# A small matrix product without a reader moves from the edge of a tile to its middle

## The chip, the cores and the metric

The kernel runs on one core of a Trainium2 chip. The metric is device time in microseconds (us) of one execution; the median of the runs before is 1422.33 us (three runs, 1422.17 to 1423.14).

## The reference

Two transformer blocks on 256 tokens of width 1024, in fp32. The parts that matter here:

```python
def first_block(...):            # attention, RG-LRU, merge, feed-forward
    xn = rmsnorm(h, norm_mix_g[l])
    u = jnp.einsum('bsd,de->bse', xn, w_in[l])
    ...
    r = jax.nn.sigmoid(jnp.einsum('bsnd,nde->bsne', xb, w_r).reshape(B, S, D) + b_r)
    i = jax.nn.sigmoid(jnp.einsum('bsnd,nde->bsne', xb, w_i).reshape(B, S, D) + b_i)
    ...
    g, up = jnp.split(hn @ w_ffn_in[l], 2, axis=-1)
    h = h + (jax.nn.silu(g) * up) @ w_ffn_out[l]
...
def swiglu(h, w_in, w_out):      # four more feed-forward layers in the second block
    gate, up = jnp.split(h @ w_in, 2, axis=-1)
    return (jax.nn.silu(gate) * up) @ w_out
```

In the second block stand, in this order, a feed-forward layer, a spatial gating unit (its `u` and `v` come out of one product, `v` is normalised and mixed over 128 tokens), two feed-forward layers, an attention with stick-breaking weights, and a last feed-forward layer.

## The kernel before

Every large product is made of three products on TensorE: weights and activations are each split into a high and a low part of type fp32r (`h`, `l` and `xh`, `xl`), and `mm3` (lines 213 to 216) adds high by high, high by low and low by high into one bank of the accumulation memory. In the trace these three are named by what they read: `xh,h`, `xl,h` and `xh,l` in the tiles that run over the input width, and `rr,h`, `rr,h`, `rr,l` where the activations lie in the tiles `rr`. Each of them is a weight load of 128x128 (engine PEld in the profile) and a matmul that streams 256 columns (engine PE). A weight tile of 128 by 1024 thus gives 24 products; a group is two tiles (`group`, line 200), 48 products.

There are five feed-forward layers, called f0 to f4 (`ffn`, line 738). Each begins with four chunks in K order (96 products) for the first two pairs of gate and up columns, then goes through the list of `ffn_order`: G2, G3, G4, R0, G5, G6, R1 and so on. G is a group of a gate tile and an up tile (`pe_a`, line 229); R is a group of two row tiles of the output product (`pe_r`, line 238). f4 makes its output in token order, with 512 columns a product (`pe_rn`). The bank of each G is read by `mulR` (line 314), which scales it on VectorE, then by silu, product and split.

The normalisation's factor comes in beside the running products: `stats_a` (line 296) sums squares with fp32 products of one column (`ones` by the tile `sb`), `stats_b` (line 305) broadcasts the factor with two fp32 products (`bcast_mm`). In f0, f2, f3 and f4 `stats_a` stands after the first tile of G2 and `stats_b` after the first tile of G3. f1 has two factors: sums after the first tile (`early`) and after the second tile (`sa`, in the trace `ones,sd`) of G2, and two broadcasts one behind the other in `sbb`.

`nudge` (line 292) is a bf16 product of 64 rows and 32 columns, of a part of an identity matrix with itself. Its result has no reader. One stands at the end of every `stats_b` (and of the second broadcast in f1), one behind the last `mix` of the spatial gating, and one wherever `due` is set when `pe_a` begins a first tile (lines 231 to 233): at G5 of every feed-forward layer (line 772), and after the last of the gate products of `lru` (line 659), which are fp32. That last one stands ahead of a tile of the first block's input product; 288 products of that kind follow it, and then a stage of 512-column products. The columns that it writes are those where the tile's own first product then starts anew.

The order on each engine is the order in which the code calls it; nothing reorders it. Banks come from two pools of four, `wk` and `acc`, in rotation: a call of `wk()` hands out the bank used four calls before, and its first writer waits for that bank's last reader. Weights come with DMAs of 1 MB on SP's queue, three ahead, and are split on ScalarE (line 163) and VectorE (line 164) up to seven tiles ahead.

Of the kernel before, what the change touches and what calls it, by code (L numbers as in the profile page):

```python
# [39 lines left out]
def ffn_order():  # L40
    seq, j, r = [("G", 2), ("G", 3), ("G", 4), ("R", 0)], 5, 1
    while j < NJ:
        for _ in range(2):
            if j < NJ:
                seq.append(("G", j))
                j += 1
        seq.append(("R", r))
        r += 1
    return seq + [("R", i) for i in range(r, NJ // 2)]
# [57 lines left out]
class Builder:  # L107
    def __init__(self, tc, dram, pools):
        self.tc, self.nc, self.dram = tc, tc.nc, dram
        self.cp, self.rawp, self.hlp, self.accp, self.wkp = pools  # L110
        self.ci = 0
        self.preps = 0
        self.loads = 0
        self.raw = {}
        self.hl = {}
        self.gens = []
        self.R = None
        self.rcol = None
        self.due = False

    @property
    def gi(self):
# [87 lines left out]
    def mm(self, out, lhsT, rhs, start, stop):  # L210
        self.nc.tensor.matmul(out, lhsT, rhs, start=start, stop=stop, skip_group_check=True)  # L211

    def mm3(self, out, wh, wl, xh, xl, start, stop):
        self.mm(out, wh, xh, start, False)
        self.mm(out, wh, xl, False, False)
        self.mm(out, wl, xh, False, stop)

    def pe_k(self, h, l, kp, xs, outs):
        XH, XL = xs
# [8 lines left out]

    def pe_a(self, h, l, xs, out, first):
        XH, XL = xs  # L230
        if first and self.due:
            self.nudge(out[:, 0:32], True)
            self.due = False
        for k in range(8):
            s = slice(k * 128, k * 128 + 128)
            self.mm3(out, h[:, s], l[:, s], XH[:, k, :], XL[:, k, :], start=(first and k == 0), stop=(k == 7))

    def pe_r(self, h, l, zh, zl, accs, first, last):
# [50 lines left out]
            self.mm(bank[:, half, t * 128:(t + 1) * 128], col[:, t:t + 1].to_broadcast([128, 128]), self.ident,  # L289
                    start and t == 0, True)  # L290

    def nudge(self, out, start=False):

        self.mm(out, self.identb[0:64, :], self.identb[0:64, 0:32], start, True)

    def stats_a(self, pool=None, kv=False):

# [316 lines left out]
    def lru(self, xr, xc, rt, it, gr, gb, ga, gw):  # L614
# [4 lines left out]
        def conv(k):  # L619
            nc.scalar.activation(xc[:, k, :], xr[:, k, 0:256], AF.Identity, bias=P("conv_b", k), scale=P("conv_w", k))  # L620
            for j in range(1, 4):
                nc.vector.scalar_tensor_tensor(xc[:, k, :], xr[:, k, j:j + 256], P("conv_w", 8 * j + k), xc[:, k, :],
                                               op0=ALU.mult, op1=ALU.add)
# [30 lines left out]
        for p in range(4):  # L654
            banks = [self.acc(), self.acc()]
            for wi in range(2):
                for f in range(2):
                    self.mm(banks[wi][:, f, :], gw[:, wi * 8 + 2 * p + f, :], xc[:, 2 * p + f, :], f == 0, True)
            self.due = p == 3
            if p < 2:  # L660
                conv(2 * p + 4)
            yield
            for f in range(2):
                k = 2 * p + f
                nc.scalar.activation(rt[:, k, :], banks[0][:, f, :], AF.Sigmoid, bias=P("b_r", k))
            yield
            if p < 2:
                conv(2 * p + 5)
            yield
            for f in range(2):  # L670
                k = 2 * p + f
                nc.scalar.activation(it[:, k, :], banks[1][:, f, :], AF.Tanh, bias=self.half[:, k:k + 1], scale=0.5)
            yield
            sl = slice(2 * p, 2 * p + 2)
            nc.vector.scalar_tensor_tensor(it[:, sl, :], it[:, sl, :], 1.0, xc[:, sl, :], op0=ALU.add, op1=ALU.mult)
# [10 lines left out]
        for i in range(2):  # L686
            s = slice(i * 1024, (i + 1) * 1024)
# [4 lines left out]
        for i in range(2):  # L692
            s = slice(i * 1024, (i + 1) * 1024)
# [44 lines left out]
    def ffn(self, n, fin, fin_l, stats=None, nat=False, more=None):  # L738
        nc = self.nc
        a, r = ("A", f"{n}_in"), ("R", f"{n}_out")  # L740
        HH, HL = self.RR[0], self.RR[1]
        tmp = [self.SA[:, i * 512:(i + 1) * 512].rearrange("p (a b) -> p a b", b=256) for i in range(4)]

        def ev(j, bank):
            t = tmp[j % 4]
            self.mulR(t, bank)
            yield
            nc.scalar.activation(t[:, 0, :], t[:, 0, :], AF.Silu)  # L748
            yield
            if nat:  # L750
                nc.vector.scalar_tensor_tensor(t[:, 1, :], t[:, 0, :], 0.5, t[:, 1, :], op0=ALU.mult, op1=ALU.mult)
            else:
                nc.vector.tensor_tensor(t[:, 1, :], t[:, 0, :], t[:, 1, :], op=ALU.mult)  # L753
            yield
            self.hl_split(t[:, 1, :], HH[:, j % 8, :], HL[:, j % 8, :])
            yield

        b = [self.wk(), self.wk()]
        self.start_k((("K", f"{n}_in"),) * 2, [b[0][:, 0, :], b[0][:, 1, :], b[1][:, 0, :], b[1][:, 1, :]],
                     ((2, 2), (0, 0)) if more else ((2, 2), (2, 2)))  # L760
        sa, sbb = stats or (self.stats_a, self.stats_b)

        def first():
            sbb()
            for j in range(3):
                self.spawn(ev(j, b[j]))

        accs = None
        for kind, i in ffn_order():
            if kind == "G":  # L770
                bank = self.wk()
                self.due = i == 5
                if i == 2:
                    b.append(bank)
                self.group((a, a), lambda c, h, l, s: self.pe_a(h, l, self.XS, bank[:, c, :], c == 0),
                           mid={2: sa, 3: first}.get(i), fills=(0, 1) if more and i < 4 else (2, 2),
                           end=more if i == 2 else lambda: self.spawn(ev(i, bank)))
            elif i < NJ // 2 - 1:
                if accs is None:
                    accs = self.ffn_accs(nat)  # L780
                self.group((r, r), lambda c, h, l, s: (self.pe_rn if nat else self.pe_r)(
                    h, l, HH[:, s[2] % 8, :], HL[:, s[2] % 8, :], accs, not nat and s[2] == 0, False))
        zf = lambda k: (HH[:, k % 8, :], HL[:, k % 8, :])
        if nat:
            self.tail_nat(f"{n}_out", (NJ - 2, NJ - 1), zf, accs, fin)
        else:
            self.tail_group(f"{n}_out", (NJ - 2, NJ - 1), zf, accs, lambda p: fin(p, accs[p]), fin_l)
# [571 lines left out]
```

## Time and profile before

| | |
|---|---|
| median of three runs | 1422.33 us |
| the profiled execution | 1422.0 us |
| its span, first to last instruction | 1420.3 us |
| mean granted TensorE clock | 0.999 |
| TensorE matmuls, busy | 1410.6 us (99%), 11564 records |
| TensorE weight loads, busy | 1368.7 us (96%), 11564 records |
| VectorE, busy | 949.8 us (67%) |
| ScalarE, busy | 735.0 us (52%) |
| DMA | 260.31 MB, 183 GB/s |

Busy time of a matmul overlaps that of the next (a record of a 256-column product lasts some 0.28 us, while the next begins much earlier), so 99% says that TensorE nearly always has work, not how fast it goes through it. How fast is read from starts: from the count of records in a stretch, or from the timeline.

### The profile page before, as it was taken

To read this page: it belongs to the slowest core of one execution; us is meant where nothing else is said; L and a number is where in the kernel's file an instruction comes from. 1 tells how busy PE (TensorE), PEld (TensorE's weight loads), DVE (VectorE), ACT (ScalarE), POOL (GpSimd) and SP (SyncE) were. 2 spreads that over 40 slices of the span, in tenths; PEclk is the share of its full clock that TensorE was granted. 3 is DMA by queue.
4 is the path that set the end of the run, shared out by engine and by line. 5 is a ranking of instruction groups with operands and counts; after the bars stand their busy time and mean duration, and the time that the engine had idled before them with its cause. 6 is when DMAs were issued, how large, how long until landed. Compare 5 with 4: busy or idle time off the path is not lost.

```text
span 1420.3 us, 26991 instructions
## 1 busy us (share of the span) xinstructions
PE 1410.6 (99%) x11564; PEld 1368.7 (96%) x11564; DVE 949.8 (67%) x1316; ACT 735.0 (52%) x1094; POOL 24.7 (2%) x57
## 2 busy tenths in 40 slices
PE   9999999999999999999999999999999999999998
PEld 9998999999999999998999999999999998999997
DVE  6976687665567666677785665667665677656663
ACT  5686465544445445455445444446544477544442
POOL 0000000000000000000000000000000000000000
PEclk9999999999999999999999999999999999999999
DMA  8555554555544555556445554454555552445551
GB/s 299 192 198 197 176 189 154 203 195 191 179 178 149 206 182 206 203 198 223 160 156 183 186 206 179 178 188 169 208 184 211 199 179 90 161 152 197 190 187 51
DMA packets 37624, 260.31 MB, mean 183 GB/s; under 512 B 4224, under 2 KB 4608, under 8 KB 7040
## 3 DMA queue, kind: packets, MB, share of 16 engines
q1 hardware_dynamic: 36288, 253.77, 50.1%
q0 software_dynamic: 1072, 4.72, 1.0%
q8 instruction: 90, 1.47, 0.4%
q14 instruction: 30, 0.25, 0.1%
q10 hardware_dynamic: 144, 0.10, 0.0%
HBM read 257.53 MB, written 1.05 MB: 182 GB/s over the span
## 4 chain that ended last, share of the span: by engine, by line
PE 98%; DMA 0%; ACT 0%; DVE 0%; SPq 0%; issue 0%; POOLq 0%; POOL 0%
PE wk L211 62%; PE acc L211 36%; DMA raw<-w 0%; PE acc L530 0%; PE wk L530 0%; ACT sf L971 0%; ACT sd L961 0%; DVE l L164 0%; ACT h L163 0%; SPq L361 0%; SPq L352 0%; DVE sf L962 0%; POOLq L1355 0%; POOL rc L284 0%; ACT sh L1148 0%
## 5 line engine op out<-in xcount | busy, mean ns | idle before, releaser
L164 DVE TENSOR_TENSOR l<-raw,h 128x1024 fp32r<-128x1024 f32 (+1 forms) x479 | 571.3, 1220 | 241.3 <-ACT h L163 240.9
L211 PE MATMUL wk<-xh,h 128*128 128x256 f32 x2272 | 637.5, 281 | 1.4 <-ACT h L163 1.4
L211 PE MATMUL wk<-xh,l 128*128 128x256 f32 x2272 | 633.5, 279 | 0.1
L211 PE MATMUL wk<-xl,h 128*128 128x256 f32 x2272 | 633.2, 279 | 0.0
L163 ACT ACTIVATE h<-raw 128x1024 fp32r<-128x1024 f32 (+1 forms) x479 | 486.3, 1046 | 61.3 <-PE acc L211 28.0
L211 PEld LDWEIGHTS wk<-xh,h 128*128 128x128 f32 x2272 | 430.8, 190 | 4.5 <-issue 2.0
L211 PEld LDWEIGHTS wk<-xh,l 128*128 128x128 f32 x2272 | 427.7, 188 | 0.5 <-DVE l L164 0.5
L211 PEld LDWEIGHTS wk<-xl,h 128*128 128x128 f32 x2272 | 427.6, 188 | 0.5
L211 PE MATMUL acc<-rr,h 128*128 128x256 f32 x2016 | 353.5, 279 | 0.0
L211 PEld LDWEIGHTS acc<-rr,h 128*128 128x128 f32 x2016 | 306.1, 189 | 2.1 <-issue 1.9
L211 PE MATMUL acc<-rr,l 128*128 128x256 f32 x1008 | 280.4, 278 | 0.0
L211 PEld LDWEIGHTS acc<-rr,l 128*128 128x128 f32 x1008 | 189.3, 188 | 0.0
L748 ACT ACTIVATE sa<-sa 128x256 f32<-128x256 f32 x110 | 45.4, 417 | 258.5 <-DVE sa L315 258.3
L318 ACT ACTIVATE rr<-sa 128x256 fp32r<-128x256 f32 (+1 forms) x122 | 52.7, 439 | 185.3 <-DVE sa L753 128.9
L315 DVE TENSOR_TENSOR sa<-wk,rt 128x512 f32<-128x512 f32 x92 | 62.4, 687 | 72.5 <-PE wk L211 54.8
L319 DVE TENSOR_TENSOR rr<-sa,rr 128x256 fp32r<-128x256 f32 (+1 forms) x122 | 54.1, 451 | 53.4 <-ACT rr L318 53.4
L211 PE MATMUL acc<-h,rr 128*128 128x512 f32 (+1 forms) x208 | 63.1, 374 | 0.0
L211 PEld LDWEIGHTS acc<-h,rr 128*128 128x128 f32 x208 | 38.5, 188 | 6.6
L262 ACT ACTIVATE xh<-x,par 128x256 fp32r<-128x256 f32 x56 | 25.0, 501 | 29.4 <-DVE x L325 16.2
L211 PE MATMUL acc<-l,rr 128*128 128x512 f32 (+1 forms) x104 | 39.0, 375 | 0.0
L753 DVE TENSOR_TENSOR sa<-sa 128x256 f32<-128x256 f32 x88 | 37.1, 429 | 0.0
L211 PE MATMUL wk<-rr,h 128*128 128x256 f32 x192 | 33.0, 277 | 0.0
(255 smaller groups left out, 972.8 us busy)
## 6 DMA issues: line engine op xcount, KB each, us to landing
raw<-w SPq DMA_DIRECT2D x237, 1024.0 KB, 5.0
sd<-bias POOLq DMA_DIRECT2D x8, 384.0 KB, 3.4
raw<-w SPq DMA_DIRECT2D x3, 512.0 KB, 7.6
sh<-gates SPq DMA_DIRECT2D x1, 1024.0 KB, 9.1
out<-sf SPq DMA_DIRECT2D x4, 256.0 KB, 2.2
x<-x SPq DMA_DIRECT2D x3, 256.0 KB, 6.6
raw<-w SPq DMA_DIRECT2D x2, 256.0 KB, 4.9
sa<-ws POOLq DMA_DIRECT2D x1, 512.0 KB, 3.8
```

The source lines that it names most:

```text
L163: nc.scalar.activation(h[:, s], raw[:, s], AF.Copy)
L164: nc.vector.tensor_tensor(l[:, s], raw[:, s], h[:, s].bitcast(F32), op=ALU.subtract)
L211: self.nc.tensor.matmul(out, lhsT, rhs, start=start, stop=stop, skip_group_check=True)
L262: self.nc.scalar.activation(xs[0][:, k, :], src[p][:, f, :], AF.Copy, scale=self.par(*g(k)))
L315: self.nc.vector.tensor_tensor(dst, bank, self.Rpair(), op=ALU.mult)
L318: self.nc.scalar.activation(zh, src, AF.Copy)
L319: self.nc.vector.tensor_tensor(zl, src, zh.bitcast(F32), op=ALU.subtract)
L748: nc.scalar.activation(t[:, 0, :], t[:, 0, :], AF.Silu)
L753: nc.vector.tensor_tensor(t[:, 1, :], t[:, 0, :], t[:, 1, :], op=ALU.mult)
```

## The change

In each feed-forward layer the small product at G5 no longer stands ahead of the tile. It stands behind the second of the tile's first three products, and writes a bank of its own, drawn from the pool `wk` ahead of the tile. The small product after the gates stays where it is and takes the fp32 identity instead of the bf16 one. Nothing else is changed.

```diff
-        self.due = False
+        self.due = 0
...
-    def mm3(self, out, wh, wl, xh, xl, start, stop):
-        self.mm(out, wh, xh, start, False)
-        self.mm(out, wh, xl, False, False)
-        self.mm(out, wl, xh, False, stop)
+    def mm3(self, out, wh, wl, xh, xl, start, stop, nudge=None):
+        for n, (w, x) in enumerate(((wh, xh), (wh, xl), (wl, xh))):
+            self.mm(out, w, x, start and n == 0, stop and n == 2)
+            if nudge and nudge[1] == n + 1:
+                self.nudge(nudge[0], True)
...
     def pe_a(self, h, l, xs, out, first):
         XH, XL = xs
-        if first and self.due:
-            self.nudge(out[:, 0:32], True)
-            self.due = False
+        if first and self.due == 3:
+            spare = self.wk()
+        elif first and self.due:
+            self.nudge(out[:, 0:32], True, self.due == 2)
+            self.due = 0
         for k in range(8):
             s = slice(k * 128, k * 128 + 128)
+            if first and self.due == 3:
+                self.mm3(out, h[:, s], l[:, s], XH[:, k, :], XL[:, k, :], True, False, (spare[:, 0, 0:32], 2))
+                self.due = 0
+                continue
             self.mm3(out, h[:, s], l[:, s], XH[:, k, :], XL[:, k, :], start=(first and k == 0), stop=(k == 7))
...
-    def nudge(self, out, start=False):
-
-        self.mm(out, self.identb[0:64, :], self.identb[0:64, 0:32], start, True)
+    def nudge(self, out, start=False, wide=False):
+
+        e = self.ident if wide else self.identb
+        self.mm(out, e[0:64, :], e[0:64, 0:out.shape[-1]], start, True)
...
-            self.due = p == 3
+            self.due = 2 if p == 3 else 0
...
-                self.due = i == 5
+                self.due = 3 if i == 5 else 0
```

## Rows read from the trace of the kernel before

**Rows 1.** The page, chain that ended last, shares of the span by engine.

```profile
PE 98%; DMA 0%; ACT 0%; DVE 0%; SPq 0%; issue 0%; POOLq 0%; POOL 0%
```

**Rows 2.** Windows: start:end and length, busy us (xrecords) by engine, PEclk, DMA.

```profile
75.00:105.00 30.00, 30.00 (x257) 30.00 (x256) 21.88 (x24) 25.85 (x35) 0.67 (x1) 1.00 0.53 184
300.00:460.00 160.00, 160.00 (x1361) 160.00 (x1360) 101.49 (x135) 74.95 (x106) 0.00 (x0) 1.00 0.52 185
490.00:625.00 135.00, 135.00 (x1194) 135.00 (x1193) 87.85 (x106) 62.68 (x86) 2.42 (x2) 1.00 0.59 213
815.00:970.00 155.00, 155.00 (x1319) 155.00 (x1318) 96.22 (x122) 73.14 (x102) 0.00 (x0) 1.00 0.52 188
1000.00:1140.00 140.00, 140.00 (x1237) 140.00 (x1237) 88.27 (x106) 64.17 (x87) 0.00 (x0) 1.00 0.55 197
```

**Rows 3.** Weight loads by form, 300 to 460 us: xcount, busy us, mean ns, idle before.

```profile
L211 PEld LDWEIGHTS wk<-xh,h 128*128 128x128 f32 x294 | 56.4, 192 | 0.0
L211 PEld LDWEIGHTS wk<-xl,h 128*128 128x128 f32 x293 | 55.0, 188 | 0.0
```

**Rows 4.** Weight loads by form, 490 to 625 us (the other two likewise 188).

```profile
L211 PEld LDWEIGHTS wk<-xl,h 128*128 128x128 f32 x254 | 47.7, 188 | 0.0
```

**Rows 5.** Weight loads, 70.5 to 72.5 us; the other two 188.

```profile
L211 PEld LDWEIGHTS wk<-xh,l 128*128 128x128 f32 x6 | 1.2, 192 | 0.0
```

**Rows 6.** Weight loads, 75 to 105 us; the other two 188.

```profile
L211 PEld LDWEIGHTS wk<-xh,h 128*128 128x128 f32 x86 | 16.5, 192 | 0.0
```

**Rows 7.** Weight loads, 275 to 279 us; the other two 188.

```profile
L211 PEld LDWEIGHTS wk<-xh,l 128*128 128x128 f32 x12 | 2.3, 192 | 0.0
```

**Rows 8.** Weight loads, 282 to 286 us; the other two 188.

```profile
L211 PEld LDWEIGHTS wk<-xh,h 128*128 128x128 f32 x12 | 2.3, 192 | 0.0
```

**Rows 9.** Weight loads, 462.5 to 464.9 us; the other two 188.

```profile
L211 PEld LDWEIGHTS wk<-xl,h 128*128 128x128 f32 x7 | 1.3, 192 | 0.0
```

**Rows 10.** Weight loads, 466 to 468 us; the other two 188.

```profile
L211 PEld LDWEIGHTS wk<-xl,h 128*128 128x128 f32 x7 | 1.3, 188 | 0.0
```

**Rows 11.** Weight loads, 471 to 474 us; the other two 188.

```profile
L211 PEld LDWEIGHTS wk<-xl,h 128*128 128x128 f32 x10 | 1.9, 188 | 0.0
```

**Rows 12.** Weight loads, 976 to 981 us; the other two 188.

```profile
L211 PEld LDWEIGHTS wk<-xl,h 128*128 128x128 f32 x15 | 2.9, 192 | 0.0
```

**Rows 13.** Weight loads, 984 to 995 us; the others 188.

```profile
L211 PEld LDWEIGHTS wk<-xh,l 128*128 128x128 f32 x19 | 3.6, 188 | 0.0
```

**Rows 14.** Timeline of PE at f0's G5: start us, length us, instruction.

```profile
294.62 0.28 PE L211 MATMUL acc<-rr,l 128*128 128x256 f32 x1
294.83 0.19 PE L211 MATMUL wk<-identb 64*128 64x32 bf16 x1
294.95 0.38 PE L211 MATMUL wk<-xh,h 128*128 128x256 f32 x1
295.17 0.28 PE L211 MATMUL wk<-xl,h 128*128 128x256 f32 x1
```

**Rows 15.** Timeline of PE, f1's two broadcasts: the second, and its small product.

```profile
468.94 0.71 PE L211 MATMUL acc<-ident,r1c 128*128 128x128 f32 x4
469.58 0.19 PE L211 MATMUL acc<-identb 64*128 64x32 bf16 x1
```

**Rows 16.** Weight loads, 232 to 270 us, ahead of f0; the others 188.

```profile
L211 PEld LDWEIGHTS wk<-xl,h 128*128 128x128 f32 x30 | 5.6, 188 | 0.0
```

**Rows 17.** Weight loads, 732 to 736 us, spatial gating; the other form 188.

```profile
L211 PEld LDWEIGHTS acc<-rr,l 128*128 128x128 f32 x12 | 2.3, 192 | 0.0
```

**Rows 18.** Weight loads, 740 to 745 us; the other form 188.

```profile
L211 PEld LDWEIGHTS acc<-rr,l 128*128 128x128 f32 x15 | 2.8, 188 | 0.0
```

**Rows 19.** Timeline of DVE ahead of f0's G5: the scaling of G4's bank.

```profile
292.74 0.68 DVE L315 TENSOR_TENSOR sa<-wk,rt 128x512 f32<-128x512 f32 x1
```

**Rows 20.** Timeline of PE: attention scores of the first block, fp32, 64 rows.

```profile
137.87 0.93 PE L211 MATMUL wk<-sb 64*128 64x128 f32 x8
```

**Rows 21.** Weight loads, 140 to 146 us, behind those; the other form 188.

```profile
L211 PEld LDWEIGHTS acc<-rr,h 128*128 128x128 f32 x37 | 5.6, 188 | 0.0
```

## The prediction

> **What bounds the kernel now.** I read the page's chain of waits first: TensorE carries 98% of it [rows 1], so only what TensorE does per product can move the end, and the question is what sets the step from one product to the next. The second view is the count of products in long stretches at full clock (PEclk 1.00 in each) [rows 2]. A record of 0.28 us overlaps a stretch's edges by 2.4 records, so the step is the stretch over (count − 2.4). The gate tiles (75 to 105 us) give 30.00/254.6 = 117.8 ns and the first feed-forward layer, f0 (300 to 460 us), 160.00/1358.6 = 117.8 ns. The next layer, f1 (490 to 625 us), gives 135.00/1191.6 = 113.3 ns, and f3 (1000 to 1140 us) 140.00/1234.6 = 113.4 ns. Same line, shapes and clock, and more DMA traffic in the quicker stretches (0.59 against 0.52): so the stream has two steps, 4.45 ns apart. f2 (815 to 970 us) goes as f0 does: 155.00/1316.6 = 117.7 ns.
>
> The third view, the weight loads by form, tells the two steps apart. In f0 the load of each tile's first product (xh,h) takes 192 ns and the others 188 [rows 3]; in f1 all take 188 [rows 4]. I name the patterns by which of a tile's three products has the long load: long-1, long-2, long-3, and even where none has. Before the gate product the stream is long-3, behind it long-1 [rows 5, 6]. Between two breaks a pattern holds for as long as 1416 products, so nothing repairs a long one but a break.
>
> So I made a list of breaks from the trace, and the pattern on either side:
> - f0's statistics: behind them long-3; after the broadcast (fp32) with its own small bf16 product, long-1 [rows 7, 8].
> - f1: the first statistics leave long-2, the second (ones,sd) leave even, and even it stays after two broadcasts with a small product each [rows 9 to 11].
> - f3: long-2 after its statistics, even after broadcast and small product [rows 12, 13].
> - The small bf16 product alone, where it stands now ahead of a tile: in f0 long-1 stays long-1 [rows 3, 8], in f1 even stays even [rows 4, 11], at the gates long-3 becomes long-1 [rows 5, 6].
>
> **The change part by part.** *The five layers.* Nothing is added or taken away in count: the same bf16 product of 32 columns goes behind the second product of tile G5. It costs now: last product 294.62, small product 294.83, second product of the tile 295.17 [rows 14], that is 0.55 us for two steps worth 0.24, so 0.31 us. Behind the second product the same drain and refill stand, so 0.00 on the sum; bounds −0.31 (it hides) to +0.31 (twice).
>
> What counts is the pattern it leaves. Say how many products ahead the next long load is: at a tile's start in long-1 that is 0, in long-3 it is 2, in long-2 it is 1. The product alone is shown for 0 (leaves 0), 2 (leaves 0) and even (leaves even). Behind the second product in long-1 the next long load is one ahead, the case that the trace never shows with the product alone. The nearest rows: in f3, long-2 (1 ahead) through an fp32 broadcast and the product gives even [rows 12, 13]. In f1, two such pairs back to back lead from even to even [rows 10, 15, 11], though one pair alone takes long-3 to long-1 in f0. Read as steps: fp32 statistics take even to 2 ahead [rows 16, 7] and 0 ahead to 1 ahead [rows 3, 9]. If the fp32 of the broadcasts does the same, the double pair is even, 2, 0, 1, even, and its last step is the product alone from 1 ahead to even. That chain closes only if 1 leads to even, so I take even; the other end is that 1 leads to another long pattern. One row speaks against such clean steps: in the gating layer, fp32 products plus the small one take long-3 to even [rows 17, 18], not to long-1.
>
> f0: from G5 to f1's statistics are 17 tile pairs of 48 products, 10 row groups of 48 and 120 of f1's first products: 1416. 1416 x 4.45 ns = 6.30 us. f2 the same: together −12.60. The other end for each is 0. What hides nothing: VectorE and ScalarE must split weights 4% faster; in f1 they did it at 87.85 and 62.68 busy us of 135 [rows 2], and DMA carried 213 GB/s there.
>
> *What follows in the next layers.* f0 would end even instead of long-1, and so would f2. Even becomes long-3 through the statistics, as at f0's own entry [rows 7, 16]. f3 would then enter as f0 does now: long-3, broadcast, long-1, for the 120 products up to G5 that are even now: 120 x 4.45 = +0.53 us; its own moved product then makes it even as in f0. f1 enters long-3, keeps that through the second statistics (24 products that are even now, +0.11 us), and the double pair should leave even as it does now. In f1 and f3 the moved product must leave even even: shown ahead of a tile, taken to hold in the middle of it, since in this pattern every load is the same. In f4 the layer mixes 512-column groups in, behind each of which the stream is even; at most the 96 products up to the next such group are at stake, ±0.43 us, taken as 0.
>
> *The spare bank.* The product now writes a bank of its own out of the rotation of four, whose last reader was the scaling of tile G2; the scaling of G4, two tiles later, begins 292.74 and lasts 0.68 us [rows 19], over 1 us ahead of G5. The wait costs 0. If G2's were still open, the third product and all behind it would wait, at most some 0.7 us a layer.
>
> *The gates.* fp32 instead of bf16: an fp32 product is two records (a broadcast's two are four [rows 15]). Eight fp32 records of 64 rows take 0.93 us with their drain [rows 20], some 0.12 each, so one more costs +0.12 (bounds 0 and +0.35). Pattern: long-3 is 2 ahead. fp32 of 128 rows made this long-3, 64-row fp32 leaves even (loads of 188 behind it) [rows 21]. The new product is fp32 and 64 rows, nearest to the last: I take even. Gain over the 288 products up to the 512-column stage: 288 x 4.45 = −1.28; other end 0.
>
> Sum: −12.60 + 0.53 + 0.11 − 1.28 + 0.12 = −13.12 us. Against the profiled execution's 1422.0 (span 1420.3 and 1.7 around it) this is 1408.9; the median of the runs is 0.33 above that execution, so the forecast is 1409.2.
>
> The Trainium skill, page "TensorE: Matmul & The Clock Gate", section "Back-to-back issue gap", gives a warm gap of columns over 2.4 GHz plus 2.5 ns, without any history: 109.2 ns for 256 columns, an estimate by that page. The trace differs, with 117.8 and 113.3 for one shape at one clock [rows 2], so the measurement decides. By its rule no placing of a product could change later steps, and the time would stay 1422.3: that is rival C's result.
>
> **The rivals.**
> A. *Layers turn, gates don't.* fp32 leaves long-3 as 128-row fp32 does: −12.60 + 0.64 + 0.12 = −11.84, 1410.5. For: the pattern ahead of the gate product, long-3, is itself what 128-row fp32 left [rows 5]. Against: [rows 21].
> B. *f0 and f2 turn, but f1 falls out.* The second statistics now meet long-3 instead of long-2, a pass the trace does not show; if the pairs behind leave f1 in long-2 or long-3, the moved product does not help and 1296 products take the longer step: +5.77, 1415.0.
> C. *The position does nothing.* f0 and f2 keep a long pattern and f1 and f3 even: 0 to +0.1, or −1.2 with the gates: 1421.2 to 1422.4. For: the product alone has healed no layer so far. Against: the same product ends pairs that heal f1 and f3.
> D. *Slower: the small product always puts the long load on the product behind it.* For: 0 and 2 ahead both end so. Then 1 ahead ends as 0 on the third product: f0 and f2 stay long and end as long-3 instead of long-1. f3's statistics no longer lead to long-2, the one entry that its broadcast turns to even, but to f0's long-1, and its moved product makes it long-3: 120 + 1392 products at the longer step, +6.73, 1429.1. If f1's entry goes the same way, 1440 more products, +6.4, 1435.5. It decides at the first tile behind f3's broadcast. Against: f1's double pair, which would have to end long by this rule.
>
> **How the numbers follow.** The forecast 0.36, A 0.25, B 0.09, C 0.10, D 0.20. The likeliest one's own range is 1408 to 1411. Leaving out D, the range is 1407.5 (0.43 in f4 and the moved product hidden in places) to 1424 (C with every unknown price on its dear side). 0.2% is 2.8 us, about what a measurement of this kernel tells from no change: faster 0.70 (forecast, A, B), same 0.10, slower 0.20.
>
> **What would show it.** Counts in 300 to 460 us near 1413 instead of 1361, and f0's loads all 188 ns: the layer step right. Loads 192 on xh,l there: rival D. f3 long-1 for 120 products ahead of G5 and even behind: the entry step right. Loads of 188 in the gate tiles from 75 us on: the gate step right; 192 on any of the three: A. A TensorE wait for the scaling's bank at G5 would break the spare bank's zero. The forecast is wrong if f0's step stays 117.8 ns, or if f1 or f3 goes to it.

## The result and the profile after

The changed kernel takes 1437.24 us (median of 4 runs, 1437.14 to 1437.98) beside 1422.74 us for the kernel before: a ratio of 1.0103, interval 1.0088 to 1.0118. That is 14.5 us slower, where 13 us less was forecast; rival D, with its second step (1435.5), came nearest.

The clock is no part of it (PEclk 1.00 in all stretches below), and TensorE still has the whole chain. Windows of the changed kernel, columns as in [rows 2]; the last stretch lies in f4:

```profile
75.00:105.00 30.00, 30.00 (x267) 30.00 (x266) 22.48 (x25) 26.13 (x36) 0.72 (x1) 1.00 0.55 193
300.00:450.00 150.00, 150.00 (x1276) 150.00 (x1275) 92.02 (x120) 65.89 (x93) 0.00 (x0) 1.00 0.52 189
490.00:625.00 135.00, 135.00 (x1149) 135.00 (x1148) 84.47 (x103) 58.98 (x81) 2.54 (x2) 1.00 0.56 201
1010.00:1140.00 130.00, 130.00 (x1106) 130.00 (x1106) 77.82 (x94) 58.17 (x79) 0.00 (x0) 1.00 0.53 188
1300.00:1400.00 100.00, 100.00 (x715) 93.97 (x714) 59.91 (x72) 44.20 (x60) 0.00 (x0) 1.00 0.52 186
```

Take the stretch over (count − 2.4) again. The gate tiles went from 117.8 to 113.4 ns. f0 stayed at 117.8. f1 went from 113.3 to 117.7 and f3 from 113.4 to 117.8 [rows 2]. f4, which mixes 256 and 512 columns, put 715 records in its 100 us; before the change it put 736 there:

```profile
1300.00:1400.00 100.00, 100.00 (x736) 94.09 (x736) 60.34 (x73) 43.37 (x60) 0.00 (x0) 1.00 0.47 169
```

Weight loads by form in the changed kernel, only the form with the long load of each stretch (the other two forms show 188). In order: f0 before G5 (284 to 293 us), f0 behind it (300 to 450), f1 between its two statistics (462 to 464), f1 between the broadcasts and G5 (470 to 482), f1 behind G5 (490 to 625), f4 (1300 to 1400):

```profile
L211 PEld LDWEIGHTS wk<-xh,h 128*128 128x128 f32 x11 | 2.1, 192 | 0.0
...
L211 PEld LDWEIGHTS wk<-xh,l 128*128 128x128 f32 x265 | 50.9, 192 | 0.0
...
L211 PEld LDWEIGHTS wk<-xh,l 128*128 128x128 f32 x6 | 1.2, 192 | 0.0
...
L211 PEld LDWEIGHTS wk<-xh,h 128*128 128x128 f32 x21 | 4.0, 192 | 0.0
...
L211 PEld LDWEIGHTS wk<-xh,l 128*128 128x128 f32 x254 | 48.8, 192 | 0.0
...
L211 PEld LDWEIGHTS wk<-xh,l 128*128 128x128 f32 x190 | 36.5, 192 | 0.0
```

This shows where f1 was lost (f3 and f4 follow below). The moved product did change f0, from long-1 to long-3, which has the same step. But long-3 goes through f1's statistics as long-3, where long-1 had become long-2 [rows 9] and then even [rows 10], and behind the broadcasts f1 is now long-1 where it was even [rows 11]. f1's own moved product then makes that long-3 as well. The timeline of PE at f0's G5 shows the product in its new place (start us, length us), to be set beside [rows 14]:

```profile
293.77 0.28 PE L211 MATMUL wk<-xh,h 128*128 128x256 f32 x1
293.89 0.28 PE L211 MATMUL wk<-xl,h 128*128 128x256 f32 x1
294.10 0.19 PE L211 MATMUL wk<-identb 64*128 64x32 bf16 x1
294.22 0.39 PE L211 MATMUL wk<-xh,l 128*128 128x256 f32 x1
294.45 0.29 PE L211 MATMUL wk<-xh,h 128*128 128x256 f32 x1
```

From the second product (293.89) to the next tile step's first (294.45) are 0.56 us for two steps: 0.32 us of detour, as before.

### The profile page after: what moved, and what is told of

The parts are those of the page before. It is cut to its first block, busy times and chain, and to the rows that moved or that the text cites. A ratio compares the mean times of both kernels' runs of the same rounds, so it can differ in the third digit from the quotient of the medians.

```text
span 1435.6 us, 26998 instructions
## 1 busy us (share of the span) xinstructions
PE 1425.3 (99%) x11565; PEld 1383.6 (96%) x11565; DVE 949.7 (66%) x1316; ACT 734.8 (51%) x1094; POOL 24.8 (2%) x57
## 4 chain that ended last, share of the span: by engine, by line
PE 98%; DMA 1%; SPq 0%; ACT 0%; DVE 0%; issue 0%; POOLq 0%; POOL 0%
PE wk L211 62%; PE acc L211 36%; DMA raw<-w 1%; PE acc L538 0%; SPq L369 0%; PE wk L538 0%; SPq L358 0%; ACT sf L979 0%; ACT sd L969 0%; DVE l L164 0%; ACT h L163 0%; SPq L360 0%; DVE sf L970 0%; POOLq L1363 0%; POOL rc L291 0%
## 5 line engine op out<-in xcount | busy, mean ns | idle before, releaser
L211 PEld LDWEIGHTS wk<-xh,l 128*128 128x128 f32 x2272 | 434.3, 191 | 1.0 <-DVE l L164 0.9
L211 PE MATMUL acc<-rr,h 128*128 128x256 f32 x2016 | 358.1, 281 | 0.0
```

## The experiments

All are variants of the two kernels; a time is a median beside runs of the kernel before on the same chip, but for e6, e7, e10 and e12, which are one run each: there the patterns in the trace are the evidence, and the time only a sign. "Ahead" is, as in the prediction, how many products ahead the next long load is where the small product comes in (0, 1 or 2), or "even".

**e1: the gate product alone.**

```diff
-                self.due = 3 if i == 5 else 0
+                self.due = 1 if i == 5 else 0
```

> Only the gate product is fp32; the five products at G5 stand ahead of their tiles in bf16 as before. Terms theory (each edit is worth what its own pattern is worth): even from 73 to 107 us, 288 products at 4.45 ns less and one record more, -1.2 us, 1421.5 against 1422.7; f0 to f4 as before, the loads of f1 and f3 all 188. Rival (fp32 at the gates carries on into the layers and is part of their loss): f1 or f3 goes to loads of 192, +6 us or more.

1421.07 against 1422.71 us, ratio 0.9989 (0.998 to 0.9998): −1.6 us. Windows of this kernel, gate tiles and f4 (f4 is as it was before the change):

```profile
1300.00:1400.00 100.00, 100.00 (x737) 94.09 (x736) 59.24 (x72) 42.36 (x58) 0.00 (x0) 1.00 0.47 169
75.00:105.00 30.00, 30.00 (x267) 30.00 (x266) 22.48 (x25) 26.01 (x36) 0.72 (x1) 1.00 0.55 191
```

All loads of the gate tiles take 188 ns. The gate edit is a gain; all the loss, 16 us, belongs to the layers.

**e2: the spare bank alone**, ahead of the tile.

```diff
-            spare = self.wk()
+            self.nudge(self.wk()[:, 0, 0:32], True)
+            self.due = 0
```

> The bf16 product at G5 stands ahead of the tile as before but writes the spare bank; gates as before. Position theory (the bank is nothing, the place in the tile is all): no change, 1422.7, patterns as before: f0 and f2 long-1, f1 and f3 even. Bank theory (the spare bank or the shifted rotation of wk costs): f1, f3 and f4 lose as in the changed kernel, about 1437.

1422.73 us, ratio 0.9999 (0.999 to 1.0008). The bank's cost is too small to see, and f0 to f4 keep the steps and patterns that they had; the theory of the bank falls.

**e3 and e4: the moved product in f0 and f2 only, and in f1 and f3 only** (gates bf16, elsewhere ahead of the tile).

```diff
-                self.due = 3 if i == 5 else 0
+                self.due = (3 if n in ("f0", "f2") else 1) if i == 5 else 0
```

> The product stands behind the second product only in f0 and f2; f1, f3, f4 and the gates as before. Entry theory (the moved product ends f0 and f2 as long-3, and the next layer's statistics and broadcast turn that into long-1, where f0's long-1 became even): f1 and f3 whole with loads of 192 on xh,l or xh,h, some 1440 and 1512 products, +13 us, 1436, with f0 and f2 no better. Own-place theory (each layer is spoilt by the product moved in it): f1 and f3 stay even, 1422.7.

> The mirror: the product stands behind the second product only in f1 and f3, which are even when they reach it. Entry theory: even stays even in the middle of a tile too, no change, 1422.7. Own-place theory: f1 and f3 go to loads of 192 behind G5, 1296 and 1392 products at 4.45 ns, +12 us, 1434.7.

e3: 1435.24 us, ratio 1.0088 (1.0074 to 1.0102), +12.5. e4: 1422.69 us, 0.9999 (0.999 to 1.0008). So f1 and f3 lose 12.5 us without any edit in them, and an edit in them alone costs nothing while they come in even. The loads of e3 in f1, between its statistics (462.9 to 465.2 us), between the broadcasts and G5 (471 to 483), behind G5 (490 to 625):

```profile
L211 PEld LDWEIGHTS wk<-xh,l 128*128 128x128 f32 x7 | 1.3, 192 | 0.0
...
L211 PEld LDWEIGHTS wk<-xh,h 128*128 128x128 f32 x22 | 4.2, 192 | 0.0
...
L211 PEld LDWEIGHTS wk<-xh,h 128*128 128x128 f32 x255 | 49.0, 192 | 0.0
```

f1 comes in long-3, is long-1 behind the broadcasts, and the product at the tile's edge leaves it there. e4's windows of f1 and f3 show that even stays even with the product in mid-tile (113.4 and 113.3 ns):

```profile
490.00:625.00 135.00, 135.00 (x1193) 135.00 (x1192) 88.74 (x107) 62.51 (x84) 2.46 (x2) 1.00 0.60 214
1010.00:1140.00 130.00, 130.00 (x1150) 130.00 (x1149) 80.79 (x98) 59.95 (x81) 0.00 (x0) 1.00 0.54 195
```

**e5: does the distance decide?** At the gates fp32 had met 2 ahead and left even. In long-1, 2 ahead is the place behind the *first* product. So f0 to f3 get an fp32 product there (the tuple is place and type; `pe_a` passes it to `mm3`), f4 the old one.

```diff
-                self.due = 3 if i == 5 else 0
+                self.due = ((0, False) if n == "f4" else (1, True)) if i == 5 else 0
```

> In f0 to f3 the product at G5 is fp32 and stands behind the first of the three products; f4 as in the kernel before, the gates fp32. Distance theory (what counts is how many products ahead the next long load is; fp32 at 2 ahead gives even, as at the gates): behind the first product of long-1 the next long load is 2 ahead, so f0 and f2 go even, -12.6; f1 and f3 then enter as long-1 (+0.64 up to G5) and go even as well; the gates -1.3, and one record more four times +0.5: 1409.9 against 1422.7. Place theory (fp32 helped at the gates because it stood between tiles): f0 and f2 stay at 117.8 ns, and f1 and f3 join them or stay, 1421 to 1435.

1410.3 us against 1422.49, ratio 0.9911 (0.9895 to 0.9928); 1409.9 was expected. Windows of f0 and f1 (113.3 and 113.4 ns), now both even:

```profile
300.00:450.00 150.00, 150.00 (x1326) 150.00 (x1325) 96.95 (x127) 70.50 (x100) 0.00 (x0) 1.00 0.53 190
490.00:625.00 135.00, 135.00 (x1193) 135.00 (x1192) 88.85 (x110) 63.12 (x88) 2.54 (x2) 1.00 0.56 202
```

The distance theory gave this number in advance; place (edge or middle of a tile) does not.

**e6 and e7: the other distances**, one run each.

```diff
+                self.due = {"f0": (0, True), "f2": (2, True)}.get(n, (0, False)) if i == 5 else 0     # e6
...
+                self.due = {"f0": (1, False), "f2": 0}.get(n, (0, False)) if i == 5 else 0            # e7
```

> A look: gates bf16; f0 has its product fp32 ahead of the tile (0 ahead, long-1), f2 has it fp32 behind the second product (1 ahead); f1, f3, f4 as before. Distance theory knows only 2 ahead to even and leaves these two open; if fp32 acted as the bf16 product does, f0 would stay long-1 and f2 would end long-3 with f3 long behind it (1430). If any fp32 product heals, both layers go even, 1410.

> A look: gates bf16; f0 has the bf16 product behind the first product, f2 has none at all at G5, f1, f3, f4 as before. Distance theory (the bf16 product always puts the long load on the product behind it): f0 becomes long-2, step 117.8 as before; f2 stays long-1 without any product, and saves its 0.31 us, f3 even as before. If f0 leaves another pattern than long-2, that theory of the bf16 product falls.

e6 took 1429.98 us. fp32 at 0 ahead left f0 long-1, at 1 ahead it left f2 long-3; f3 behind it was long (117.8 ns), as expected. Its long loads in f0 (300 to 450 us) and f2 (815 to 965):

```profile
L211 PEld LDWEIGHTS wk<-xh,h 128*128 128x128 f32 x265 | 50.9, 192 | 0.0
...
L211 PEld LDWEIGHTS wk<-xh,l 128*128 128x128 f32 x265 | 50.9, 192 | 0.0
```

e7 took 1429.54 us. bf16 behind the first product left f0 long-2, and f2 without any stayed long-1 through 1536 products. What I had not expected: f0's long-2 passes f1's first statistics as even and the second as long-3, so f1 became long (the whole kernel +7 us). Its long loads in f0 (300 to 450 us) and in f1 behind the second statistics (467 to 469):

```profile
L211 PEld LDWEIGHTS wk<-xl,h 128*128 128x128 f32 x265 | 50.9, 192 | 0.0
...
L211 PEld LDWEIGHTS wk<-xh,l 128*128 128x128 f32 x6 | 1.2, 192 | 0.0
```

**e8: fp32 ahead of G4, no bf16 products at the broadcasts** (`push` is set outside the feed-forward layers only).

```diff
+                self.due = (0, True) if i == 4 else (0, False) if i == 5 and n == "f4" else 0
...
-        self.nudge(self.st[:, 0, 64:96])
+        if push:
+            self.nudge(self.st[:, 0, 64:96])
...
-            self.nudge(st1[:, 1, 0:32])
```

> The best version that the theory points to: in the feed-forward layers the bf16 products of the broadcasts go; an fp32 one stands ahead of G4, 24 products behind the broadcast; G5 has none except in f4 (bf16 as before); gates fp32. If the broadcast's fp32 leaves long-3 as long-3, as the mixing's products do, the fp32 product at G4 meets 2 ahead, as at the gates, and f0 to f4 are even from there: -12.6 in f0 and f2, -0.85 for two entries from G4 on instead of G5, f1 and f3 about +0.5, gates -1.3, and 5 bf16 products of 0.31 us less: about 1408 against 1422.7. If the broadcast alone leaves another pattern, the layers stay long behind G4, 1420 to 1440.

1426.8 us, ratio 1.0029 (1.0018 to 1.004): the gain missed. Its long loads in f0 ahead of the broadcast (274 to 278 us), between broadcast and G4 (280 to 282) and behind G4 (300 to 450):

```profile
L211 PEld LDWEIGHTS wk<-xh,l 128*128 128x128 f32 x12 | 2.3, 192 | 0.0
...
L211 PEld LDWEIGHTS wk<-xl,h 128*128 128x128 f32 x6 | 1.2, 192 | 0.0
...
L211 PEld LDWEIGHTS wk<-xh,h 128*128 128x128 f32 x265 | 50.9, 192 | 0.0
```

The broadcast alone takes long-3 to long-2, not to long-3 as the statistics do. fp32 then met 1 ahead and left 0, as in e6. f1's two bare broadcasts likewise took even to long-2, and so did the one of f4. The form with the long load behind f1's broadcasts (468.5 to 470.8 us); f4 ahead of its broadcast, where all forms show 188 (1248 to 1252), and behind it (1253.5 to 1255.5):

```profile
L211 PEld LDWEIGHTS wk<-xl,h 128*128 128x128 f32 x7 | 1.3, 192 | 0.0
...
L211 PEld LDWEIGHTS wk<-xh,h 128*128 128x128 f32 x13 | 2.4, 188 | 0.0
...
L211 PEld LDWEIGHTS wk<-xl,h 128*128 128x128 f32 x6 | 1.2, 192 | 0.0
```

**e9: the same behind the second product of G4**, where long-2 is 2 ahead.

```diff
-                self.due = (0, True) if i == 4 else ...
+                self.due = (2, True) if i == 4 else ...
```

> As the version with fp32 at G4 and bare broadcasts, but the fp32 product stands behind the second of the three products. Distance theory: the bare broadcast leaves long-2 in f0, f2 and f4 (and by its two other readings in f3 and f1 too), so behind the second product the next long load is 2 ahead and fp32 gives even: f0 to f4 even from G4 on. Against the version with fp32 behind the first product at G5 (1410.3): 96 products a layer at 4.45 ns less, -0.43 each in four layers, and six bf16 products of 0.31 us less, -1.9: about 1406.8. If the theory fails for a place so soon behind a broadcast, the layers stay long as ahead of G4, about 1427.

1407.79 us against 1422.64, ratio 0.9894 (0.9878 to 0.9911); 1406.8 was expected. f0 to f4 are even from G4 on. The window of f0 (113.3 ns), and f1's long loads ahead of its two bare broadcasts (458.5 to 461 us) and behind them (462.3 to 464.9):

```profile
300.00:450.00 150.00, 150.00 (x1326) 150.00 (x1325) 97.53 (x127) 71.09 (x101) 0.00 (x0) 1.00 0.54 192
...
L211 PEld LDWEIGHTS wk<-xh,l 128*128 128x128 f32 x7 | 1.3, 192 | 0.0
...
L211 PEld LDWEIGHTS wk<-xl,h 128*128 128x128 f32 x8 | 1.5, 192 | 0.0
```

So the bare double broadcast ends long-2 from long-3 as it did from even.

**e10 and e12: 128 rows instead of 64**, one run each. e10 has fp32 in f0 and bf16 in f2, both at 2 ahead; e12 has bf16 at 0 ahead in f0 and at 1 ahead in f2.

```diff
+                self.due = {"f0": (1, True, 128), "f2": (1, False, 128)}.get(n, (0, False)) if i == 5 else 0    # e10
...
+                self.due = {"f0": (0, False, 128), "f2": (2, False, 128)}.get(n, (0, False)) if i == 5 else 0   # e12
```

> A look at which property heals at 2 ahead: both products behind the first product at G5, of 128 rows instead of 64, fp32 in f0 and bf16 in f2; gates bf16, f1, f3, f4 as before. If fp32 is what heals: f0 even, f2 long-2. If the 64 rows are what heals: f0 goes as fp32 of 128 rows went in the statistics (2 ahead stays 2 ahead, long-1 again for the tile order) and stays at 117.8 ns; f2 open. Healed f0 alone: -6.3 with f1's entry long (f1 then long-1 through the bf16 product ahead of G5, +6.4).

> A look that fills the table for the bf16 product of 128 rows: in f0 ahead of the tile (0 ahead), in f2 behind the second product (1 ahead); gates bf16 of 64 rows, f1, f3, f4 as before. If the form heals from everywhere: f0 and f2 even, 1416 products each less 4.45 ns, with f1 and f3 entering long: about 1422. If the distance decides as for fp32: f0 and f2 stay at 117.8 ns, f0's end decides f1, f2's end f3: 1422 to 1436.

e10 took 1422.15 us, and neither of my readings held: both forms healed. Its windows of f0, f1 and f2, 113.3, 117.7 and 113.3 ns:

```profile
300.00:450.00 150.00, 150.00 (x1326) 150.00 (x1325) 97.33 (x127) 70.27 (x100) 0.00 (x0) 1.00 0.53 191
490.00:625.00 135.00, 135.00 (x1149) 135.00 (x1148) 83.67 (x102) 60.45 (x83) 2.48 (x2) 1.00 0.54 196
820.00:960.00 140.00, 140.00 (x1238) 140.00 (x1237) 89.59 (x112) 66.35 (x94) 0.00 (x0) 1.00 0.53 189
```

The time is unchanged because f1 (row 2) and f3 (117.8 ns) lost what f0 and f2 won. e12 took 1422.4 us: at 0 ahead f0 went even, at 1 ahead f2 stayed long (the long load 1 ahead again, on the first product). Its window of f0 (113.3 ns) and its long loads in f2 (815 to 965 us):

```profile
300.00:450.00 150.00, 150.00 (x1326) 150.00 (x1325) 97.51 (x127) 70.28 (x100) 0.00 (x0) 1.00 0.54 191
...
L211 PEld LDWEIGHTS wk<-xh,h 128*128 128x128 f32 x265 | 50.9, 192 | 0.0
```

Again neither reading held in full: the distance decides for this form too, but otherwise than for fp32.

**e11: e9 with bf16 of 128 rows**, which is cheaper.

```diff
-                self.due = (2, True) if i == 4 else ...
+                self.due = (2, False, 128) if i == 4 else ...
...
-            self.due = (0, True) if p == 3 else 0
+            self.due = (0, False, 128) if p == 3 else 0
```

> The version with fp32 behind the second product of G4 (1407.8), with the five products at G4 and the one at the gates as bf16 of 128 rows. The look before showed this form at 2 ahead in f2: the layer went even, and the detour was 124 + 38 + 200 ns for two steps of 118 (0.13 us) where the fp32 one of 64 rows took 211 + 132 + 203 + 222 (0.53 us). Distance theory: the same patterns, six detours 0.40 us shorter, 1405.4. If the 128-row form healed f2 for another reason than its distance, some layer stays at 117.8 ns, 1411 or more.

1404.86 us against 1423.03, ratio 0.9872 (0.9856 to 0.9889); 1405.4 was expected. It is 18 us below the kernel before and the best of all. The timeline of PE at f0's G4:

```profile
281.38 0.28 PE L211 MATMUL wk<-xl,h 128*128 128x256 f32 x1
281.50 0.19 PE L211 MATMUL wk<-identb 128*128 128x32 bf16 x1
281.54 0.36 PE L211 MATMUL wk<-xh,l 128*128 128x256 f32 x1
281.74 0.28 PE L211 MATMUL wk<-xh,h 128*128 128x256 f32 x1
```

From 281.38 to 281.74 are 0.36 us for two steps, where the bf16 product of 64 rows took 0.56: 0.13 us of detour. The small product starts one plain step (0.12 us) behind the product ahead of it; the one of 64 rows started 0.21 us behind [rows 14].

## Why the prediction was wrong

**The failing step.** It was "That chain closes only if 1 leads to even, so I take even". The bf16 product of 64 rows meets 1 ahead and leaves 0: f0 behind G5 is long-3 in the changed kernel and in e3. The case was taken from a chain of steps of which one, the broadcast by itself, had never been seen alone. The chain let it act as the statistics do, even to 2 ahead. e8 and e9 show it bare: it takes even to long-2 and long-3 to long-2. The chain also took it that only this pattern counts for what comes next. Without the small products f1's double broadcast ends long-2 from even (e8) and from long-3 (e9); with them it ends even from even [rows 10, 11] and long-1 from long-3 (the changed kernel). So beside fp32 products the small product does not act on that pattern as it does behind plain products; whether the one between the two broadcasts or the one behind them makes the difference, no run separates. The row quoted against clean steps [rows 17, 18] had said as much: there fp32 products and a small one end even from long-3, where the small product behind plain products leaves 2 ahead long (e7).

**f0 and f2, forecast −12.60: 0.** They changed from long-1 to long-3 and kept their step.

**f1 and f3, forecast +0.64: +12.5** (e3). Rival D worked this out: 1440 + 1512 products at 4.45 ns, 13.1. The entry decides. Of the four patterns in which f0 can end, long-1 alone led to even in f1 (long-2 did not in e7, long-3 not in e3, even not in e10). In f3 long-1 led to even, and even and long-3 did not; long-2 is not run. A second reading of the forecast failed here: "the double pair should leave even as it does now". From long-3 it leaves long-1, in e5 too, where f0 did end even (f1 between its broadcasts and G5, 463.5 to 477 us):

```profile
L211 PEld LDWEIGHTS wk<-xh,h 128*128 128x128 f32 x24 | 4.6, 192 | 0.0
```

So even with f0 and f2 healed, f1 and f3 would have needed a product of their own that clears a long pattern, and the moved one does not. For f3 the forecast had this entry right.

**f4, forecast 0 with ±0.43: about +3.6**, what is left of 14.5 when +12.5 and −1.6 are taken out. The traces agree: from the last weight load of G4 to that of the last G tile are 146.07 us before (1256.12 to 1402.19) and 149.62 after (1267.88 to 1417.50), 3.55 more. It is f4's own product that costs this: up to G5 f4 has the same patterns in both kernels (long-3 behind the statistics, long-1 behind the broadcast), and in e3, where f3 was long and f4's product unmoved, f4 lost nothing (737 records). The bound rested on "behind each 512-column group the stream is even". f4's groups of 24 such products do not make it even, they pass on what was there: even stays even before the change, and long-3 now lasts to the end of f4 (715 records instead of 736). What pattern G5 met there can't be read, since only two plain products stand between a 512-column group and the small product; that stays open.

**The gates, forecast −1.16: −1.6** (e1), inside e1's interval. The size came out right, in part by luck. 2 ahead did heal, but the 64 rows were not needed, since fp32 of 128 rows heals at 2 ahead as well (e10). And [rows 21] could not show a healing: ahead of those 64-row products the stream was even already (129.3 to 137.6 us of the kernel before, all forms 188):

```profile
L211 PEld LDWEIGHTS wk<-xl,h 128*128 128x128 f32 x16 | 3.0, 188 | 0.0
```

**The rest held**: the detour (0.32 us against 0.31), the spare bank with no cost to be seen (e2), even staying even in mid-tile (e4), and VectorE, ScalarE and DMA keeping up when f0 ran at 113.3 ns (e5).

## What to carry to other kernels

Where one engine has the whole chain, divide stretches by counts before anything else: one instruction form with two steps at one clock is a pattern that something sets and something else could clear, here worth 0.9% of the time in e5 (the 1.3% of e11 hold fewer and cheaper small products too). Write down what each kind of break does to each pattern only where it was seen, and do not multiply entries: the table of a break is good for the place it was read in. An edit that changes no step where it stands can still decide a stage far behind it, so follow what it leaves up to the next break that clears everything.

## What the runs showed of the hardware

What a 32-column product leaves, by how many products ahead the next long load is. An entry counts the same way from the product right behind it (0 is that product). All stand behind plain products, in the kernels named; e6, e7, e10 and e12 are one run each; "not run" where none has it:

| | even | 0 ahead | 1 ahead | 2 ahead |
|---|---|---|---|---|
| bf16, 64 rows | even (e4) | 0 (before) | 0 (after) | 0 (e7) |
| fp32, 64 rows | even (e8's f3) | 0 (e6) | 0 (e6, e8) | even (e1, e5, e9) |
| bf16, 128 rows | not run | even (e12) | 1 (e12) | even (e10, e11) |
| fp32, 128 rows | not run | not run | not run | even (e10) |

The step of 113.3 or 117.8 ns goes with loads of 188 ns or one of 192 in three; it holds for over 1500 products, came out the same in each layer that was entered the same way, and moves with neither bank (e2) nor traffic (DMA share 0.53 at 113.3 ns in e5's f0, 0.56 at 117.7 ns in the changed kernel's f1). Why the engine has two steps, and why 64 rows of bf16 cleared the longer one at none of the three distances, no run here tells: the table is what was seen, not a mechanism.
